# Context v of three heads by seven quarter products, and modulation sums by ScalarE and accumulating transfers

## The chip, the cores and the metric

The kernel runs on one core of a Trainium2 chip. The metric is device time in microseconds (us) of one execution. The engines of the core are named as the profile names them: PE (TensorE, the matmuls, with PEld for its weight loads), DVE (VectorE), ACT (ScalarE), POOL (GpSimd, which here only issues transfers) and SP (SyncE, which issues transfers too). Each engine takes its own instructions in order and waits for the others by semaphores.

## The reference, cut to what matters

Two layers over 512 latent tokens `x` and 256 context tokens `ctx`, of width 1024. Layer 0 is a bidirectional retention mixer with four heads, layer 1 a gated MLP in chunks. Each layer first normalizes its tokens and modulates them with a shift and a scale; a gate multiplies its output.

```python
shift_x, scale_x, gate_x = jnp.split(silu_c @ ada_w[i] + ada_b[i], 3, axis=-1)
hx = rmsnorm(x, norm_g[i]) * (1 + scale_x[:, None]) + shift_x[:, None]
hc = rmsnorm(ctx, norm_g[i]) * (1 + scale_c) + shift_c

def retention_project(h, w_in):
    q = to_heads(h @ w_in[:, :a], RET_HEADS)
    k = to_heads(h @ w_in[:, a:bq], RET_HEADS) * (RET_QK_DIM ** -0.5)
    v = to_heads(h @ w_in[:, bq:cq], RET_HEADS)
    z = h @ w_in[:, cq:]
```

Per head, q and k have 256 columns, v and z 512. For the latent tokens all four are computed, for the context tokens only k and v (the context's own output is needed by no later layer). The output is the latent stream after a final RMSNorm.

## The kernel before

**Precision.** A float32 matrix is held as a pair of fp32r tiles, high and low part: ACT casts the high part, DVE subtracts it from the source for the low part (`split`). One product of two such pairs is three matmuls (`mm3`: low x high, high x low, high x high).

**Quads and seven products.** The retention projections are done in quads: a matrix of weights cut into 2 x 2 quarters, against the tokens' matrix `A` cut the same way (512 tokens by 1024 features). A quad is computed by the Strassen-Winograd form: seven products of quarters in place of eight, with sums of weight quarters (built by DVE, in `Stream.sum`) and sums of token quarters (`S1` to `S4`, built once). The order in a quad is `SINGLE` = B11, T1, T2, B21, T3, B22, T4. `Product.run` runs one of them; the results are put together by ACT copies (`snap`) and DVE additions (`plus`), and `done` gets each finished quarter of the result. A latent product is 24 matmuls of 128x128 weights with 256 moving columns.

Twelve quads stand in `QUADS`. `("kq", h)` is k and q of a head; there the weights' tiles are what PE loads and the tokens move (`features`). `("vz", h, f)` is half f of the columns of v beside half f of z; there the tokens are loaded and the weights move (`tokens`). The first three quads (head 0) are done ahead; the loop at the end of the projection, `for n, q in enumerate(QUADS[3:])`, runs the other nine, n = 0 to 8: vz 1 (two), kq 1, vz 2 (two), kq 2, vz 3 (one), kq 3, vz 3 (one).

**The context.** `Product.beside` multiplies all 256 context tokens (`hc`) by the two raw quarters B11 and B21 of a quad: the left column of quarters, which is k in a kq quad and v in a vz quad. That is a plain product, 24 more matmuls behind each of B11 and B21.

**Weights.** `Stream` loads raw quarters (two transfers of 256 KB each, issued by SP) into seven slots, `w0` to `w6`, and makes the pairs two products ahead (`Q.get`) in four `hl` tiles.

**Order.** PE keeps the order of the text (`pe.kept`). In the projection loop ACT, DVE, SP and POOL have no written order; each queue's order is settled when the program is built. Work called by `aside` is pinned behind the instruction that stands before it in the text on ACT and DVE.

**The modulation of later stages** is computed in the background (`background`, one `step` per call): four pieces, i = 0 to 3, each a row vector `silu(c) @ W` with `W` 1024 x 1024. `ada_piece` loads eight rows of 128x1024 (512 KB each) into two buffers in turn, and DVE multiplies each by its column of `cpad` and adds it into `ada_a`. Its steps are one per row (nine in all), then an empty one; in the next, `columns` has PE sum over partitions (`pst<-ada_a,ones`), and one more finishes the piece. The first three pieces are done in the projection loop; before, a step follows each product except those of i = 2 and 4, from n = 0 on. The fourth follows during attention.

**Other names.** `between_modes` is one small float32 matmul of ones, put between two kinds of quads. `later` holds the finishing of k and q (rotation by `rope`, then `spill`), popped one at a time after some products. `spill` is a transfer to DRAM issued by POOL. `t2` are eleven buffers of 128x512 for snapshots. `decay` builds a head's decay table with Exp on ACT; head 0's is made in the loop at n = 5.

Of the kernel before, what the change touches and what calls it, by code (L numbers as in the profile page):

```python
# [13 lines left out]
P = 128  # L14
# [53 lines left out]
def hybrid_kernel(ctx, tc, xT_d, cT_d, cv_d, sv_d, rows_d, ada0_d, adag_d, w_d, rope_d, dec_d, ws_d, id_d, out_d):  # L68
# [86 lines left out]
    class Stream:  # L155
# [40 lines left out]
        def upto(self, n, late=None):  # L196

            while self.done < min(n, self.limit or len(self.items)):
# [4 lines left out]
                hl = place() if place else hl_tile(q[0] in ("vz", "v1"))  # L203
# [60 lines left out]
    def parts_of(q, u):  # L264
# [5 lines left out]
        if kind == "vz":  # L270
            return wide_parts(16 * i + (8 if nh else 4), kh, q[2])
        if kind == "v1":
            return wide_parts(64 + 4 * i, kh, nh)
# [4 lines left out]
    QUADS = (("kq", 0), ("vz", 0, 0), ("vz", 0, 1), ("vz", 1, 0), ("vz", 1, 1), ("kq", 1), ("vz", 2, 0), ("vz", 2, 1),  # L278
             ("kq", 2), ("vz", 3, 0), ("kq", 3), ("vz", 3, 1))
# [11 lines left out]
    for q in QUADS[3:]:  # L291
        Q.quad(q, SINGLE)
        for u in RAWS:
            Q.load((q, u), W, 1, parts_of(q, u))
# [79 lines left out]
    class Product:  # L374
# [3 lines left out]
        def __init__(self, product, done, side=None, z="tm"):  # L378
            self.product, self.done, self.side, self.z_tag, self.s = product, done, side, z, {}

# [9 lines left out]
        def beside(self, name, w):  # L390
# [5 lines left out]
            else:  # L396
                self.product(self.c, self.side[:, :, 4:8, :], w, False)
                self.done("c", self.c)

        def run(self, name, w):  # L400
# [22 lines left out]
            if name in ("B11", "B21"):  # L423
                self.beside(name, w)

# [211 lines left out]

    def project(q):
        if q[0] == "kq":
            return Product(features, kq_done(q[1]), hc)  # L640
        return Product(tokens, vz_done(q[1], q[2]), hc)
# [197 lines left out]

    spot = [0]  # L840
# [41 lines left out]
    def background():  # L882
        for i in range(4):
            a = None
            for a in ada_piece(i, *(("g1", ("g2", "g3")) if i < 3 else ("oA22", ("w2", "w3")))):
# [78 lines left out]
    def load_qk(h):  # L964
        tags = ("s0", "s1", "s2", "s3", "w4") if h % 2 == 0 else ("rope", "w5", "w6", "g2", "g3")
# [15 lines left out]
    def load_wo(h):  # L981
        raws = []
        for c in range(4):
            for j in range(len(raws), min(c + 2, 4)):
                raws.append(st([P, 1024], ("w0", "w7")[j % 2], name="raw"))
# [44 lines left out]
    dec0 = decay(0, ("g0", "s3"))  # L1030
# [607 lines left out]
```

## Time and profile before

| | |
|---|---|
| median of three timed runs | 871.4 us (870.92 to 871.57) |
| span of the profiled execution, first to last instruction | 869.6 us |
| transfers' queue 1 (issued by SP), share of the 16 DMA engines | 43.7% |
| transfers' queue 0 (issued by POOL) | 8.2% |

The profile gives the span of one execution; it has no time of its own beyond that, and the 1.8 us between the span and the median lie ahead of the first and behind the last instruction, or are the difference between executions. In the views, a row of a timeline is start, duration, engine, line, operation, tiles (out<-in), shape and count, with the idle time before it in brackets; a row of a group is count, busy time, mean ns of one and idle time before; a row of windows is, for each engine, busy us and instructions, then PE's clock, the DMA engines' share and GB/s; a row of DMA issues ends with the median us from issue to landing. Nearly all instructions carry line 54, that of a helper, so groups are told apart by tiles. `hl` are the pairs of weights, `oA` and `oS` those of latent tokens and their sums, `hc` those of the context.

### The profile page before, as it was taken

Reading aid. Unit: us, or ns where it says so; the run is one execution under the profiler, and the core shown is the slowest. Engines: PE = TensorE matmul, PEld = TensorE weight load, DVE = VectorE, ACT = ScalarE, POOL = GpSimd, SP = SyncE. Lnnn points to the kernel's source line nnn. Section 1 sums busy time; section 2 is a strip of 40 time slices with the busy share of each in tenths; the row PEclk is TensorE's granted clock in tenths of the full one; section 3 lists DMA queues with packets and bytes.
Section 4 is the critical chain, followed back from the end, with each engine's and each line's share of the span. In section 5 each row is a group of like instructions: output and inputs, shape, how many; then the busy total and the mean of one; then the engine's idle time right before and its main releaser. Section 6 shows DMA issues by size and latency. Waiting matters only on the chain.

```text
span 869.6 us, 16989 instructions
## 1 busy us (share of the span) xinstructions
PE 860.9 (99%) x6898; PEld 824.1 (95%) x6898; DVE 715.0 (82%) x1004; ACT 458.5 (53%) x711; POOL 58.3 (7%) x96
## 2 busy tenths in 40 slices
PE   8999999999999999999999999999999999999997
PEld 7899999999999999999989899999999899899986
DVE  4799988699789777878676679999899488688995
ACT  5476644435544346627363549744666456255434
POOL 0001210101102011000000002011000000000110
PEclk9999999999999999999999999999999999999999
DMA  9943887557567467746164602635435035035522
GB/s 359 404 152 109 256 279 254 170 181 242 203 213 256 132 219 302 267 165 241 66 222 141 215 4 110 211 117 206 135 122 193 26 122 203 16 122 170 120 46 102
DMA packets 74238, 153.81 MB, mean 177 GB/s; under 512 B 7728, under 2 KB 32816, under 8 KB 74160
## 3 DMA queue, kind: packets, MB, share of 16 engines
q1 hardware_dynamic: 65856, 128.40, 43.7%
q0 software_dynamic: 7872, 24.12, 8.2%
q8 instruction: 54, 0.88, 0.4%
q14 instruction: 24, 0.20, 0.1%
q10 hardware_dynamic: 432, 0.20, 0.1%
HBM read 128.58 MB, written 24.12 MB: 176 GB/s over the span
## 4 chain that ended last, share of the span: by engine, by line
PE 95%; DMA 3%; DVE 1%; ACT 0%; issue 0%; SPq 0%; DVEq 0%; ACTq 0%
PE pst L54 95%; DMA ada_w<-in_ada_dram 2%; DMA xs<-in_xT_dram 1%; DVE o L54 0%; ACT junk L54 0%; SPq L54 0%; ACT fss L54 0%; ACT o L54 0%; DVE fss L54 0%; ACT oA L54 0%; DVE oA L54 0%; DVE xs L54 0%; DVEq L1634 0%; DVE gs L54 0%; DVE ada_s L54 0%
## 5 line engine op out<-in xcount | busy, mean ns | idle before, releaser
L54 DVE TENSOR_TENSOR hl<-raw,hl 128x1024 fp32r<-128x1024 f32 (+2 forms) x197 | 235.4, 1199 | 65.9 <-ACT hl L54 65.3
L54 ACT CAST hl<-raw 128x1024 fp32r<-128x1024 f32 (+2 forms) x197 | 203.0, 1034 | 137.9 <-DVE raw L54 55.8
L54 PE MATMUL pst<-hl,oS 128*128 128x256 f32 x1152 | 133.9, 277 | 0.0
L54 PEld LDWEIGHTS pst<-hl,oS 128*128 128x128 f32 x1152 | 132.4, 188 | 0.4 <-issue 0.4
L54 PE MATMUL pst<-oS,hl 128*128 128x256 f32 x1104 | 132.5, 277 | 0.0
L54 PEld LDWEIGHTS pst<-oS,hl 128*128 128x128 f32 x1104 | 128.1, 188 | 0.8 <-issue 0.8
L54 PE MATMUL pst<-oA,hl 128*128 128x256 f32 x936 | 116.5, 279 | 0.1
L54 PEld LDWEIGHTS pst<-oA,hl 128*128 128x128 f32 x936 | 110.6, 188 | 2.3 <-issue 0.8
L54 DVE TENSOR_TENSOR raw<-raw 128x1024 f32<-128x1024 f32 x92 | 111.8, 1219 | 0.8
L54 ACT COPY snap<-pst 128x512 f32<-128x512 f32 x92 | 53.7, 584 | 92.7 <-PE pst L54 92.4
L54 PE MATMUL pst<-hl,oA 128*128 128x256 f32 x768 | 92.4, 277 | 0.0
L54 PE MATMUL pst<-og,hl 128*128 128x256 f32 x768 | 91.1, 278 | 0.0
L54 PEld LDWEIGHTS pst<-og,hl 128*128 128x128 f32 x768 | 89.2, 188 | 0.3
L54 PEld LDWEIGHTS pst<-hl,oA 128*128 128x128 f32 x768 | 89.4, 188 | 0.0
L54 PE MATMUL pst<-v,ph 128*128 128x512 f32 x192 | 59.8, 393 | 0.0
L54 PE MATMUL pst<-hl,ya 128*128 128x512 f32 (+1 forms) x246 | 59.1, 386 | 0.0
L54 PEld LDWEIGHTS pst<-hl,ya 128*128 128x128 f32 x246 | 45.3, 188 | 9.5
L54 DVE TENSOR_TENSOR snap<-pst,snap 128x512 f32<-128x512 f32 x69 | 47.3, 685 | 5.3 <-PE pst L54 5.3
L54 PE MATMUL pst<-hl,hc 128*128 128x256 f32 x384 | 46.1, 276 | 0.0
L54 PEld LDWEIGHTS pst<-hl,hc 128*128 128x128 f32 x384 | 44.7, 188 | 0.0
L54 ACT CAST ph<-pf 128x512 fp32r<-128x512 f32 x24 | 14.8, 618 | 54.5 <-DVE pf L54 54.1
L54 PEld LDWEIGHTS pst<-v,ph 128*128 128x128 f32 x192 | 36.1, 188 | 7.1
(186 smaller groups left out, 1022.7 us busy)
## 6 DMA issues: line engine op xcount, KB each, us to landing
raw<-in_w_dram SPq DMA_DIRECT2D x224, 256.0 KB, 4.1
bg<-in_adag_dram SPq DMA_DIRECT2D x32, 512.0 KB, 3.9
ada_w<-in_ada_dram SPq DMA_DIRECT2D x16, 512.0 KB, 8.7
raw<-in_w_dram SPq DMA_DIRECT2D x16, 512.0 KB, 4.3
bg<-in_dec_dram SPq DMA_DIRECT2D x12, 512.0 KB, 4.8
v<-snap POOLq DMA_DIRECT2D x16, 256.0 KB, 5.5
z<-snap POOLq DMA_DIRECT2D x16, 256.0 KB, 4.7
v<-v SPq DMA_DIRECT2D x8, 512.0 KB, 3.4
```

The source lines that it names most:

```text
L54: made = op(*args, **kw)
```

## The change

- The quads of heads 1 to 3 are cut otherwise: `("v", h)` is all 512 columns of v and `("z", h)` all of z, in place of two quads with half of each. The number of quads stays. Their order in the loop is kq 1, v 1, z 1, kq 2, v 2, z 2, v 3, z 3, kq 3.
- For these heads the context's v is computed in the seven-product form as well (`along`): context quarters `CA` of 128 tokens by 512 features, with their sums from `ctx_sums` (in the first quad of the loop), 12 matmuls behind each of the seven latent products of a v quad. The context's k, and v of head 0, stay as they were.
- `ada_piece` no longer adds on DVE. The first row is loaded into `ada_a` itself; ACT scales each row in place by its column of `cpad`; from the second row on, a transfer issued by POOL adds the row into `ada_a` (`accum_op=ALU.add`).
- Steps of the background follow every product from n = 1 on. Slots, tags and the places of `between_modes`, `later` and head 0's loads are moved to match: the weight slots `w4` and `w5` give way to `s0` and `s2`.

```diff
-    QUADS = (("kq", 0), ("vz", 0, 0), ("vz", 0, 1), ("vz", 1, 0), ("vz", 1, 1), ("kq", 1), ("vz", 2, 0), ("vz", 2, 1),
-             ("kq", 2), ("vz", 3, 0), ("kq", 3), ("vz", 3, 1))
+    QUADS = (("kq", 0), ("vz", 0, 0), ("vz", 0, 1), ("kq", 1), ("v", 1), ("z", 1), ("kq", 2), ("v", 2), ("z", 2), ("v", 3),
+             ("z", 3), ("kq", 3))
+    W2 = [w for w in W if w not in ("w4", "w5")] + ["s0", "s2"]
...
+        def along(self, name, w):
+
+            at, out = self.ctx
+            if name == "B11":
+                self.c, self.c_lo = pt(), t2("ctx")
+            elif name == "T1":
+                self.cz, self.c_hi = pt((P, HS)), t2("ctx")
+            bank = self.cz if name in ("T1", "B22") else self.c[:, HS:] if name == "B21" else self.c[:, 0:HS]
+            a = at[WITH[name]]
+            for kt in range(4):
+                r = (w[:, 0, kt * HS:kt * HS + HS], w[:, 1, kt * HS:kt * HS + HS])
+                mm3(bank, (a[:, 0, kt, :], a[:, 1, kt, :]), r, name in ("B11", "T1") and kt == 0, kt == 3)
+            lo, hi = ((t[:, 0:HS], t[:, HS:]) for t in (self.c_lo, getattr(self, "c_hi", self.c_lo)))
+            if name == "B11":
+                act.copy(lo[0], bank)
+            elif name == "T1":
+                act.copy(hi[1], bank)
+            elif name == "T2":
+                act.copy(lo[1], bank)
+            elif name == "B21":
+                dve.tensor_tensor(lo[0], bank, lo[0], ALU.add)
+            elif name == "B22":
+                dve.tensor_tensor(lo[1], bank, lo[1], ALU.add)
+                spill(out[:, 0, :], self.c_lo)
+            elif name == "T3":
+                dve.tensor_tensor(hi[1], bank, hi[1], ALU.add)
+            else:
+                act.copy(hi[0], bank)
+                spill(out[:, 1, :], self.c_hi)
...
+    def ctx_sums():
+        (x0, x1), (y0, y1) = ((c[:, :, 0:P], c[:, :, P:]) for c in cq)
+        dve.tensor_tensor(y1, x1, y1, ALU.add)
+        dve.tensor_tensor(shc, sh0[:, 0:4, 1], sh0[:, 4:8, 1], ALU.add)
+        t = ctx_tile("S1", "s1")
+        for k in range(4):
+            shifted(y1[:, k, :], shc[:, k:k + 1], t[:, 0, k, :], t[:, 1, k, :])
+        yield
+        dve.tensor_tensor(y1, y1, x0, ALU.subtract)
+        t = ctx_tile("S2", "w4")
+        for k in range(4):
+            shifted(y1[:, k, :], sh0[:, 4 + k, 1:2], t[:, 0, k, :], t[:, 1, k, :])
+        yield
...
@@ ada_piece
             if k < KT:
-                rows.append(bg_raw(tags))
+                rows.append(a if k == 0 else bg_raw(tags))
                 load(rows[k], adag_d[8 * i + k])
-            if k == 0:
-                yield None
-                continue
-            r, c = rows[k - 1], cpad[:, k - 1, 0:1]
-            if k == 1:
-                dve.tensor_scalar(a, r, c, None, ALU.mult)
-            else:
-                dve.scalar_tensor_tensor(a, r, c, a, ALU.mult, ALU.add)
+            if k:
+                r = rows[k - 1]
+                act.activation(r, r, AF.Copy, scale=cpad[:, k - 1, 0:1])
+                if k > 1:
+                    nc.gpsimd.dma_start(a, r, accum_op=ALU.add)
             yield None
...
     for n, q in enumerate(QUADS[3:]):
         pr = project(q)
-        if n in (0, 3, 6, 8):
+        if n in (1, 4, 6):
             inside_t.append(between_modes)
-        if n == 5:
+        if n == 3:
             inside.append(between_modes)
         for i, name in enumerate(SINGLE):
             pr.run(name, Q.get())
-            if i in (1, 5) if n == 0 else i % 2:
+            if i in (1, 5) if n == 0 else i % 2 or (n, i) == (8, 6):
                 popped()
-            if 2 not in pieces and i not in (2, 4):
+            if n == 0 and i % 2 == 0:
+                next(ctx_sum)
+            if n and 2 not in pieces:
                 pieces.append(step())
             if n == 5 and i % 2 == 0:
                 aside(dec0)
-            if n == 8 or (n == 6 and i < 3):
+            if n == 8 or (n == 7 and i < 3):
                 aside(qk0)
```

The finishing of v and z quarters follows the new quads (`wide_done`): of a v quad only the last quarter is copied by ACT, of a z quad all four get their SiLU there, the last one into a buffer of `t2`.

More of the change, by code (lines that the diff above doesn't have):

```diff
@@ L202, in upto @@
                 self.sum(self.done)
-                hl = place() if place else hl_tile(q[0] in ("vz", "v1"))
+                hl = place() if place else hl_tile(q[0] in ("vz", "v", "z", "v1"))
                 split((hl[:, 0, :], hl[:, 1, :]), r, late)
@@ L293, in hybrid_kernel @@
         for u in RAWS:
-            Q.load((q, u), W, 1, parts_of(q, u))
+            Q.load((q, u), W2, 1, parts_of(q, u))
     PROJECTED = len(Q.items)
@@ L837, in sum_s3, with ctx_tile @@
         kept_in("S3", f11)
+    shc = st([P, 4], "shb", name="shc")
+    def ctx_tile(key, tag):
+        CA[key] = st([P, 2, 4, P], tag, F32R, name="cs")
+        return CA[key]
+    def ctx_sums():
[11 more added lines that the diff above has]
+        yield
+        dve.tensor_tensor(y0, y0, y1, ALU.subtract)
+        t = ctx_tile("S4", "w5")
+        split((t[:, 0], t[:, 1]), y0)
+        yield
+        dve.tensor_tensor(x0, x0, x1, ALU.subtract)
+        t = ctx_tile("S3", "g3")
+        split((t[:, 0], t[:, 1]), x0)
+        yield
     spot = [0]
@@ L1029, in hybrid_kernel @@
     Q.free.remove("g0")
-    dec0 = decay(0, ("g0", "s3"))
+    Q.free += ["s0", "s2"]
+    Q.pump()
+    dec0 = decay(0, ("g0", "w7"))
+    ctx_sum = ctx_sums()
     pieces = []
```

32 lines of the change are left out of this document (26 added, 6 removed).

## The prediction

> **What bounds the kernel now.** I read the page first, then the projection stage, where the whole change lies, in three views: the table of windows, the timeline of weight loads, and the groups of instructions.
>
> ```profile
> span 869.6 us, 16989 instructions
> PE 860.9 (99%) x6898; PEld 824.1 (95%) x6898; DVE 715.0 (82%) x1004; ACT 458.5 (53%) x711; POOL 58.3 (7%) x96
> ...
> 67.00:330.00 263.00, 263.00 (x2319) 261.38 (x2318) 226.51 (x274) 127.26 (x164) 36.95 (x58) 1.00 0.64 214
> ```
>
> TensorE is busy 99% of the span. The third row is the stretch from 67 to 330 us: 263.00 of 263.00 us on PE, clock 1.00, DVE 226.51, ACT 127.26. Nothing that DVE, ACT or a transfer does there is seen by PE. So the time can fall only by matmuls that go, and it rises by whatever makes PE wait, us for us.
>
> ```profile
> 107.49 2.79 PEld L54 LDWEIGHTS pst<-hl,hc 128*128 128x128 f32 x24
> 110.21 5.51 PEld L54 LDWEIGHTS pst<-hl,oS 128*128 128x128 f32 x48
> 115.65 2.79 PEld L54 LDWEIGHTS pst<-hl,oA 128*128 128x128 f32 x24
> ...
> 151.01 2.79 PEld L54 LDWEIGHTS pst<-hl,oA 128*128 128x128 f32 x24
> 153.73 2.89 PEld L54 LDWEIGHTS pst<-oA,hl 128*128 128x128 f32 x24
> 156.56 2.90 PEld L54 LDWEIGHTS pst<-hc,hl 128*128 128x128 f32 x24
> 159.59 0.16 PEld L54 LDWEIGHTS pst<-ada_a,ones 128*32 128x32 f32 x8
> ```
>
> One product of a quad is 24 matmuls and takes 2.72 us from start to start (107.49 to 110.21), so 113.3 ns each. The row at 159.59 is `columns` of the first modulation piece: PE reads `ada_a` there, in the order of the text, with no wait.
>
> **The change, part by part.**
>
> *Context products.* Before, each of the two v/z quads of a head multiplies all the context by two v quarters: 2 x 24 matmuls, so 96 a head. After, seven products of 12 matmuls make 84. Three heads: 36 fewer, 36 x 113.3 ns = **-4.1 us**. These lie on the path.
>
> *Two smaller PE terms.* The loop has four `between_modes` matmuls in place of five.
>
> ```profile
> 179.46 0.78 PEld L54 LDWEIGHTS pst<-hl,oA 128*128 128x128 f32 x6
> 180.16 0.31 PEld L54 LDWEIGHTS pst<-ones 128*128 128x128 f32 x2
> 180.39 2.13 PEld L54 LDWEIGHTS pst<-hl,oA 128*128 128x128 f32 x18
> ```
>
> One takes 0.23 us (180.16 to 180.39): -0.2. But the feature quad behind a token quad at 153.73, which got none, ran its first 24 in 2.83 us, 0.11 more. After the change the quads kq 1 and kq 3 get none, 216 matmuls each: between 0 and 2 x 9 x 0.11 = 2.0 us; I take +1.0, as the columns' matmuls may end the effect early. Matmuls in all: **-3.3 us**.
>
> *Evacuation and the context's sums.* A head's two 512-wide ACT copies of context v give way to four 256-wide ones and three 256-wide DVE additions; `ctx_sums` adds seven 512-wide operations and sixteen small ones, over both engines, in the first quad of the loop.
>
> ```profile
> L54 DVE SCALAR_TENSOR_TENSOR ada_a<-bg,cpad,ada_a 128x1024 f32<-128x1024 f32 x28 | 35.8, 1279 | 0.6 <-DMA bg<-in_adag_dram 0.6
> ...
> L54 DVE TENSOR_TENSOR xs<-xs 128x512 f32<-128x512 f32 x8 | 5.2, 686 | 0.0
> ...
> L54 DVE SCALAR_TENSOR_TENSOR oS<-xs,shb,oS 128x256 fp32r<-128x256 f32 x4 | 1.7, 484 | 0.6 <-ACT oS L54 0.6
> ```
>
> On DVE that is five at 0.69 and eight at 0.48 or less: at most 7.3 us, in a quad that no longer has its five modulation steps of 1.28 us. DVE's slack hides it; price on PE 0. If that cover went, PE would lose the excess, about 1 us. Later quads lose all modulation work on DVE, which buys nothing, since PE waits for DVE nowhere here.
>
> *The modulation sums.* This is the term that decides. Before, step k of a piece was one DVE operation of 1.28 us. After, it is a scaling on ACT (k from 1 to 8) and, from the second on, a transfer by POOL that adds the row into `ada_a`: seven a piece, each writing the tile that the one before it writes. The weight rows still have two buffers, and a buffer is free for the next load only when its adding transfer has landed. Nothing in the trace is a 512 KB adding transfer. The nearest rows are:
>
> ```profile
> o<-x POOLq DMA_DIRECT2D x8, 256.0 KB, 4.0
> ...
> bg<-in_adag_dram SPq DMA_DIRECT2D x32, 512.0 KB, 3.9
> ...
> v<-v SPq DMA_DIRECT2D x8, 512.0 KB, 3.4
> ...
> DMA to landing us min/median/max: 3.8/4.0/5.5
> ...
> q0 software_dynamic: 1152, 2.10, 25.4%
> ...
> L54 ACT CAST hl<-raw 128x1024 fp32r<-128x1024 f32 x191 | 200.3, 1051 | 137.9 <-DVE raw L54 55.8 <-PE pst L54 51.9 <-issue 15.2
> ...
> L54 ACT CAST qk<-qk 128x512 fp32r<-128x512 f32 x20 | 12.4, 618 | 0.0
> ...
> L54 ACT ACTIVATE bg<-bg,lg 128x512 f32<-128x512 f32 x24 | 15.7, 715 | 11.4 <-DMA bg<-in_dec_dram 11.3
> ```
>
> The adding transfers `o<-x` at the end of the kernel move 256 KB and land after 3.8 to 5.5 us, 4.0 in the median. The q0 row is the window 800 to 850 us: these eight (2.10 MB) held all 16 DMA engines for 25.4% of 50 us, 12.7 us, so 1.6 us each. Twice the bytes add 1.6 us: estimate **5.6 us** per transfer. Below, no 512 KB transfer's median is under the 3.4 us of `v<-v`; above, the largest `o<-x` plus 1.6 us is 7.1. I take 5.6, from the nearest row, the one other adding transfer. The scaling of 1024 elements is estimated at 1051 + (715 - 618), so 1.15 us.
>
> Seven in a row take 7 x (5.6 + 0.1) = 39.9 us. The buffers give nearly the same: a round of transfer 5.6, load 3.9, scaling 1.15 and some 0.2 for handing over is 10.85 us for two rows; three rounds and the last transfer are 38.2. I use **40 us** from the first adding transfer until the piece is whole.
>
> How long has it? A step follows each product from quad n = 1 on. The first adding transfer belongs to step 2 of a piece and PE's `columns` to step 10. With token products of v at 36 x 113.3 ns = 4.08 us and all others at 2.72:
> - piece 1: four products of v 1 and four of z 1: 16.3 + 10.9 = 27.2 us
> - piece 2: the rest of kq 2 (19.0), half a doubled product ahead of it (2.7), two of v 2 (8.2): 29.9 us
> - piece 3: two of v 2 (8.2; its scaling stands behind a cast, not an evacuation, so nearly a product earlier) and all of z 2 (19.0): 27.2 us
>
> The scaling itself and the issue take 1.4 us off each: 25.8, 28.5, 25.8. PE takes its instructions in the order of the text, so it waits at `columns` for 40 less that: 14.2 + 11.5 + 14.2 = **+39.9 us**. At 3.4 us a transfer (buffers: 3 x 8.65 + 3.4 = 29.4) the waits are 3.6 + 0.9 + 3.6 = 8.1; at 7.1 us (7 x 7.2 = 50.4) they are 24.6 + 21.9 + 24.6 = 71.1. The fourth piece has its steps spread over attention, three to six a head, and costs nothing.
>
> A rule bears on this. The Trainium skill ("DMA: Bandwidth & Descriptors", section "Anatomy of one DMA — SWDGE (gpsimd) path") fits such a transfer at 2.0 us plus bytes over 436 GB/s, which for 256 KB is an estimate of 2.6 us and for 512 KB of 3.2; the trace's 4.0 for 256 KB of adding speaks against it here. By that figure the sum would be about +2.
>
> What is queued behind these waits: POOL holds the spills of q, k, v and z behind each adding transfer, so each may start up to 5.6 us late, and its `t2` buffer is held as long; eleven such buffers, of which I count eight or nine in use in v 1, hide that. SP holds the weight loads behind each row load. That is covered:
>
> ```profile
> SPq L54 <- DVE ada_a L54: 84.7, 22, 13.2
> ...
> L54 ACT COPY snap<-pst 128x512 f32<-128x512 f32 x92 | 53.7, 584 | 92.7 <-PE pst L54 92.4
> ...
> L54 ACT ACTIVATE snap<-snap 128x512 f32<-128x512 f32 x16 | 10.1, 630 | 12.0 <-DVE snap L54 12.0
> ...
> L54 ACT ACT_TABLE_LOAD x16 | 20.5, 1283 | 1.9 <-PEq L1627 1.7
> ```
>
> SP, in the view of its own waits from 60 to 345 us, already stood up to 13.2 us at a time for `ada_a`, and PE lost nothing. ACT gets 24 x 1.15 = 28 us in the loop and has 136 us of slack in the window quoted above; its tight place is a rival below, worked out from the last three rows and those of the casts and exponentials above.
>
> **Sum.** -3.3 + 39.9 = +36.6 us: the profiled span goes from 869.6 to 906.2. The median of the three timed runs is 871.4, 1.8 us above the span, so the prediction is **908.0 us**.
>
> **Rivals.**
> - *As short as a plain transfer.* Adding costs nothing over moving, 3.4 us: +8.1 - 3.3 = +4.8, so 876.2. For it: the source lies in SBUF, not in HBM. Against it: 4.0 us for half the bytes. The figure of the Trainium skill's page named above belongs to this case and would make it about 874 (an estimate: 3 x 8.45 + 3.2 = 28.6 us a piece).
> - *ACT becomes the bound in z 2.* Quad z 2 has 19.0 us on PE. ACT has seven casts (7.4), three snaps (1.8), four SiLUs (2.5), five scalings (5.8), six exponentials of `decay` (4.3), and SiLU and Exp in turn need some four table loads at 1.28 (5.1): 26.9 us. The excess of 7.9, less a lead of one to two products (2.7 to 5.4), costs 2.5 to 5.2; with the chain of transfers barely late, about 880. For it: before, decay shared a quad with kq, with no SiLU inside. Against it: alone it is small, and a PE that waits for `ada_a` gives ACT the time anyway.
> - *The chain is hidden; faster.* If a piece is whole in 26 to 28 us, PE never waits and only the matmuls count: 871.4 - 3.3 = **868.1**. It decides at 7 x 3.7 = 25.9, so a transfer of 3.7 us, with loads near their fastest as well. Against it: no row of an adding transfer is below 3.8, at half the size.
> - *Much longer under load.* The DMA engines are 0.64 busy in the window quoted first; a row more costs some 3.2 us of them (twice 1.6), which may stretch loads and transfers to 7.1 us: +71.1 - 3.3, so 939.
>
> **How the numbers follow.** The waiting chain near 5.6 us: 0.52. Longer, up to 939 and a little beyond: 0.10. As short as a plain transfer: 0.12. ACT as the bound: 0.08. Hidden: 0.14 faster by over 0.2% (about 1.7 us, what a measurement here can tell from no change), and 0.04 within. So 0.14, 0.04 and 0.82. The range reaches from the hidden case, 867, to 7.1 us a transfer, 940: it leaves out some 0.1.
>
> **What would show it.** In the timeline of PE's weight loads: three waits of 11 to 14 us ahead of `pst<-ada_a` and none elsewhere in the loop; adding transfers `ada_a<-bg` at 5 to 6 us to landing, with POOL waiting between them; SP waiting for those transfers; 36 fewer context matmuls at 113 ns. If the adding transfers land in under 3.8 us, or POOL sends them without waiting for each other and the row loads are ahead, the chain falls, and so does the forecast. If PE waits for `hl` instead, ACT's order is the cause.

## The result, and the profile after

The changed kernel takes 969.9 us (median of four runs, 964.74 to 970.34) where the kernel before takes 871.2 (870.92 to 871.57): a ratio of 1.1117, interval 1.1091 to 1.1143. The forecast was 908.0 us, range 867 to 940. The direction was right, the size was not.

The head of the page after, then the same stretch of 263 us as before in the table of windows:

```profile
span 968.6 us, 17017 instructions
PE 877.4 (91%) x6860; PEld 836.3 (86%) x6860; DVE 689.7 (71%) x996; ACT 499.2 (52%) x760; POOL 82.5 (9%) x124
```

```profile
67.00:330.00 263.00, 197.10 (x1634) 193.90 (x1632) 160.57 (x210) 123.68 (x157) 45.59 (x64) 0.87 0.71 201
```

PE, full before, is busy for 197.10 of 263.00 us and its clock falls to 0.87 there. DVE and ACT are less busy than before too (160.57 for 226.51; 123.68 for 127.26). So no engine became the bound; the engines wait for something that is none of them. PE's waits say for what (us in total, times, longest):

```profile
PE pst L54 <- DMA ada_a<-bg: 61.7, 3, 28.7
PE pst L54 <- ACT snap L54: 6.9, 2, 5.0
PE pst L54 <- DVE pl L54: 6.1, 2, 5.1
PE pst L54 <- DVE snap L54: 4.0, 2, 2.9
```

Three waits, 61.7 us together, are at `columns`. Here is each of the first three pieces of the modulation: POOL's row of its first adding transfer, then PE's row of its `columns` (start, duration; the bracket is the idle time before):

```profile
147.16 0.88 POOL L939 DMA_DIRECT2D ada_a<-bg  x1
...
213.79 0.92 POOL L939 DMA_DIRECT2D ada_a<-bg  x1 [3.41 <-ACT bg L54]
...
276.99 0.91 POOL L939 DMA_DIRECT2D ada_a<-bg  x1 [1.73 <-ACT bg L54]
```

```profile
196.88 1.08 PE L54 MATMUL pst<-ada_a,ones 128*32 128x256 f32 x8 [18.12 <-DMA ada_a<-bg]
...
262.78 1.08 PE L54 MATMUL pst<-ada_a,ones 128*32 128x256 f32 x8 [14.85 <-DMA ada_a<-bg]
...
337.00 1.08 PE L54 MATMUL pst<-ada_a,ones 128*32 128x256 f32 x8 [28.70 <-DMA ada_a<-bg]
```

From the first of seven adding transfers to `columns` it took 49.7, 49.0 and 60.0 us: 7.1, 7.0 and 8.6 us for each row. The time to landing of all 28, in the view of line 939:

```profile
DMA to landing us min/median/max: 4.5/6.7/11.4
```

**Where the 99.0 us of the span went** (968.6 less 869.6). PE's idle time over the whole span rose by 99.0 - 16.5 = 82.5 us, since its busy time rose by 16.5 (877.4 less 860.9). Of this, 61.7 is at `columns` and 20.8 is elsewhere. PE's timeline has most of the second part: 9.8 us in the loop behind ACT's late rows (waits of 5.00 and 1.93 for ACT, and 2.85 for a DVE that had itself waited for ACT), 6.1 for `pl` in attention, 2.3 for `acc`, and 1.2 for DVE at the start of the loop. The largest of those in the loop:

```profile
171.45 4.59 PE L54 MATMUL pst<-hl,oS 128*128 128x256 f32 x24 [5.00 <-ACT snap L54]
```

The busy time rose although 38 matmuls are gone (6898 less 6860; 4.3 us at 113.3 ns), so the others took 16.5 + 4.3 = 20.8 us longer; that this is 20.8 once more is chance. Most of it is the clock: PE's busy time in windows of 1 us, each times what the granted clock lacks to 1.00 there, adds up to 16.0 us (0.0 before). The rest, 4.8, we read as the pace shown under the first experiment. The windows around the first wait, and PE's timeline behind it:

```profile
180.00:197.00 17.00, 0.12 (x4) 0.15 (x8) 8.33 (x10) 3.85 (x5) 3.55 (x5) 0.55 0.92 255
197.00:207.00 10.00, 10.00 (x69) 9.19 (x69) 3.83 (x6) 2.30 (x4) 0.69 (x1) 0.74 0.42 139
```

```profile
197.90 5.00 PE L54 MATMUL pst<-hl,oS 128*128 128x256 f32 x24
202.74 0.38 PE L54 MATMUL pst<-ident,cole 128*128 128x128 f32 x2
```

The clock fell to half while PE stood, and stayed there when work came back: the first 24 matmuls took 4.84 us from start to start (197.90 to 202.74) in place of 2.72, and the ten microseconds behind the wait ran at 0.74. This wait cost its length and then some 2.6 us more (10 x 0.26). The Trainium skill ("TensorE: Matmul & The Clock Gate", section "Part 1: The HAM clock gate (the "warmup" mystery)") has the clock go to half after an idle window of about 3.4 us and back after a busy one of that length; the trace agrees with it in kind, but doesn't show the figure itself: in windows of 0.5 us the clock is at half from 181.6 to 202.2 us, so it fell some 2.9 us after PE's last matmul (178.8) and came back some 5.3 us after PE went on (196.9).

### The profile page after: what moved, and what is told of

The parts are those of the page before. It is cut to its first block, busy times and chain, and to the rows that moved or that the text cites. A ratio compares the mean times of both kernels' runs of the same rounds, so it can differ in the third digit from the quotient of the medians.

```text
span 968.6 us, 17017 instructions
## 1 busy us (share of the span) xinstructions
PE 877.4 (91%) x6860; PEld 836.3 (86%) x6860; DVE 689.7 (71%) x996; ACT 499.2 (52%) x760; POOL 82.5 (9%) x124
## 5 line engine op out<-in xcount | busy, mean ns | idle before, releaser
L54 PE MATMUL pst<-hl,oS 128*128 128x256 f32 x1152 | 141.3, 284 | 6.9 <-ACT snap L54 6.9
L54 PEld LDWEIGHTS pst<-hl,oS 128*128 128x128 f32 x1152 | 138.7, 194 | 8.9 <-ACT snap L54 7.3
L54 PE MATMUL pst<-oA,hl 128*128 128x256 f32 x936 | 119.3, 283 | 2.9 <-DVE snap L54 2.9
L54 PEld LDWEIGHTS pst<-oA,hl 128*128 128x128 f32 x936 | 113.4, 192 | 4.8 <-DVE snap L54 3.0
L54 PE MATMUL pst<-hl,oA 128*128 128x256 f32 x768 | 96.0, 282 | 1.4 <-DVE snap L54 1.2
L54 PEld LDWEIGHTS pst<-hl,oA 128*128 128x128 f32 x768 | 92.6, 192 | 2.7 <-ACT hl L54 1.3
L54 ACT COPY snap<-pst 128x512 f32<-128x512 f32 x80 | 46.5, 583 | 60.4 <-PE pst L54 60.3
L54 ACT ACTIVATE bg<-bg,cpad 128x1024 f32<-128x1024 f32 x28 | 32.2, 1152 | 65.5 <-DMA bg<-in_adag_dram 65.3
L54 PE MATMUL pst<-ada_a,ones 128*32 128x256 f32 x24 | 3.2, 631 | 61.7 <-DMA ada_a<-bg 61.7
L54 PE MATMUL pst<-v,pl 128*128 128x512 f32 x96 | 39.2, 408 | 6.1 <-DVE pl L54 6.1
```

Source lines behind the costliest of these rows:

```text
L54: made = op(*args, **kw)
```

## The experiments

Two theories stood at the start. *Theory 1*, the prediction's: the time lies in the chain of adding transfers that PE waits for, and the context products are a small gain. *Theory 2*: ACT now scales the rows in its own order, so late rows hold up the casts and evacuations that stand behind them; the transfers are one way to make rows late. All kernels below are the changed kernel with the edit that is shown, unless another base is named; `...` in an edit stands for lines left out. Times from single runs are given without an interval; the kernel before took 871.3 to 871.9 us in the median beside each.

### The two halves of the change alone

`ctx_only` keeps the context products and puts the sums back on DVE, with their rows:

```diff
-                rows.append(a if k == 0 else bg_raw(tags))
+                rows.append(bg_raw(tags))
...
-                act.activation(r, r, AF.Copy, scale=cpad[:, k - 1, 0:1])
-                if k > 1:
-                    nc.gpsimd.dma_start(a, r, accum_op=ALU.add)
+                dve.scalar_tensor_tensor(a, r, c, a, ALU.mult, ALU.add)
```

> The modulation sums go back to DVE operations (a multiply and seven multiply-adds a piece, rows in two buffers); everything else is as after the change. Theory 1 (the chain of adding transfers makes PE wait at columns, and nothing else of the change costs): the three waits ahead of pst<-ada_a of 18.1, 14.9 and 28.7 us go, with the clock loss behind them, and the time is that of before less the matmul terms, 866 to 869 us, ratio 0.994 to 0.998. Theory 2 (the new context products or their evacuation make PE wait too): 875 us or more, with waits ahead of hl,cs or hl,hc.

884.06 us (882.62 to 885.23), ratio 1.0146 [1.0132, 1.016]. The half that was to gain 3.3 us costs 12.5. It isn't the context products alone, though. The change puts a step of the modulation behind every product, and here each step that has a row is a DVE operation of 1.28 us: up to seven a quad, where before had up to five and the changed kernel has none on DVE. PE's and DVE's timelines where the first loss lies:

```profile
176.07 1.08 PE L54 MATMUL pst<-ada_a,ones 128*32 128x256 f32 x8 [4.17 <-DVE snap L54]
```

```profile
173.00 0.68 DVE L54 TENSOR_TENSOR rope_a<-pst,rope 128x512 f32<-128x512 f32 x1
...
174.20 1.22 DVE L54 TENSOR_TENSOR hl<-raw,hl 128x1024 fp32r<-128x1024 f32 x1
175.34 0.68 DVE L54 TENSOR_TENSOR snap<-pst,snap 128x512 f32<-128x512 f32 x1
```

`columns` waits 4.17 us, and `ada_a` isn't what it waits for: the releaser is a `snap` addition that empties a PSUM bank (where matmuls leave their results), and it stands on DVE behind rotations and a `hl`. (`columns` takes a bank of the tag that quads use; that this bank is the one that `snap` left is read from the code.) It lies in z 1, where a product lasts 2.7 us and no context matmul follows, so DVE has less time to catch up than in v 1; DVE works there without a pause from 162.8 us on, and two of the modulation's multiply-adds are in that stretch. The second part of the loss is the pace. In the timeline of weight loads, 24 matmuls in this kernel and in `ctx_modes`, an experiment further down:

```profile
230.84 2.90 PEld L54 LDWEIGHTS pst<-hl,oS 128*128 128x128 f32 x24
233.67 1.49 PEld L54 LDWEIGHTS pst<-hl,cs 128*128 128x128 f32 x12
```

```profile
230.25 2.79 PEld L54 LDWEIGHTS pst<-hl,oS 128*128 128x128 f32 x24
232.97 1.44 PEld L54 LDWEIGHTS pst<-hl,cs 128*128 128x128 f32 x12
```

The first pair is of `ctx_only`, the second of `ctx_modes`: 2.83 us against 2.72, so 118 ns a matmul against 113. This is a token quad, and the transposes of piece 2's `columns` lie just ahead of it (225.87 us): without a `between_modes` behind them the slow pace holds for quads on end, here over some 140 us of the loop, which makes some 5 us (0.11 in each 2.83). With the waits (4.17, and 1.15 and 1.39 in two other places), 2.9 us of lower clock (counted as above) and 4.3 us of matmuls saved, that is some 10.7; the loop ended 11.0 us later than before (first `pst<-qk` at 340.92 for 329.90).

`sums_only` is the other half: the kernel before with the new modulation sums, rows and all.

```diff
-                rows.append(bg_raw(tags))
+                rows.append(a if k == 0 else bg_raw(tags))
...
-                dve.scalar_tensor_tensor(a, r, c, a, ALU.mult, ALU.add)
+                act.activation(r, r, AF.Copy, scale=cpad[:, k - 1, 0:1])
+                if k > 1:
+                    nc.gpsimd.dma_start(a, r, accum_op=ALU.add)
```

> The kernel before with the modulation sums alone by ScalarE and adding transfers; its steps stay at five of seven products, from n = 0 on. Between step 2 and step 10 PE then has about 11 products of 3.5 us, 39 us, in place of 26 to 28. Theory 1 (a chain of 49 us a piece against PE's time between those steps): three waits of about 10 us ahead of pst<-ada_a, some 10 us more of clock and of the fourth piece, 905 to 920 us. Theory 2 (ACT's load, table loads included, is the cause, not the chain): the SiLU and Exp no longer meet in one quad, so little is lost, 875 us or less.

931.92 us, above what either theory expected, and PE's waits show why theory 1 isn't all:

```profile
PE pst L54 <- ACT snap L54: 17.6, 4, 6.5
PE pst L54 <- DMA ada_a<-bg: 12.4, 3, 6.0
```

With the steps spread as before the change, PE waits for `ada_a` only 12.4 us in three places, and yet the kernel loses 60. It waits longer for ACT, 17.6 us.

### Theory 2: ACT behind late rows

`late_columns` gives each of the first three pieces six more steps before PE reads it:

```diff
             yield
+            for _ in range(6 if i < 3 else 0):
+                yield
             if i == 0:
```

> After the change, with six empty steps put ahead of columns in each of the first three pieces, so that PE reads ada_a six products later; the transfers are the same. Theory 1: six products are 19 us or so, and the chain needs 22 more than it has: the waits ahead of pst<-ada_a fall from 18.1, 14.9 and 28.7 us to under 10 in all, and 875 to 890 us remain, of which 8 us are attention's waits on the fourth piece. Theory 2 (ACT stands behind late rows and keeps back the casts that PE needs): PE waits for hl or snap in the loop instead, and the time stays above 930 us.

924.42 us, between the two theories. No wait at `ada_a` is left, and the time is still 53 us above that of before. ACT's timeline, then PE's, then ACT's waits:

```profile
167.25 1.05 ACT L54 CAST hl<-raw 128x1024 fp32r<-128x1024 f32 x1
170.86 1.15 ACT L54 ACTIVATE bg<-bg,cpad 128x1024 f32<-128x1024 f32 x1 [2.55 <-DMA bg<-in_adag_dram]
171.91 0.57 ACT L54 COPY snap<-pst 128x512 f32<-128x512 f32 x1
```

```profile
172.53 4.38 PE L54 MATMUL pst<-hl,oS 128*128 128x256 f32 x24 [5.83 <-ACT snap L54]
```

```profile
ACT bg L54 <- DMA bg<-in_adag_dram: 73.3, 15, 8.5
```

ACT stands 2.55 us for a row of weights; the copy that empties a PSUM bank stands behind the scaling; PE waits 5.83 us for that copy. The row was late since its buffer was still being read by an adding transfer: that one was issued at 161.23 us and landed 5.7 us later, the row's load was issued at 167.0 and landed 3.8 us later. The changed kernel has the same sequence at its wait of 5.00 us. So the chain of transfers reaches PE by two ways, and taking away one leaves the other.

### What of it is adding, what is moving, what is ACT

`add_on_dve` keeps ACT's scaling and adds on DVE; no adding transfer is left. `plain_copy` keeps the transfers and lets them overwrite (the additions are left out).

```diff
-                    nc.gpsimd.dma_start(a, r, accum_op=ALU.add)
+                    dve.tensor_tensor(a, a, r, ALU.add)
```

> After the change, with each transfer ada_a<-bg replaced by a DVE addition of the scaled row into ada_a; ACT still scales. Theory 1 (the transfers' chain is what costs; ACT's scaling as such does not): as the context change alone, 882 to 890 us. Theory 2 (ACT's extra 28 us of scaling, with the table loads in z 2, holds back PE's casts even when the rows come in time): 900 us or more, with PE waiting for hl or ACT snap.

```diff
-                    nc.gpsimd.dma_start(a, r, accum_op=ALU.add)
+                    nc.gpsimd.dma_start(a, r)
```

> After the change, with the transfers ada_a<-bg as plain copies; the additions of the modulation sums are left out (only the last row stays). Theory A (adding is what makes these transfers long, by the engine time that the o<-x rows show): they land in 3.5 to 4.5 us in the median in place of 6.7, the chain shrinks to about 33 us, and the waits at columns fall to some 5, 3 and 12 us, 895 to 905 us. Theory B (traffic beside them and the hand-over on POOL's queue): they still land in 5.5 us or more, and the time stays above 935 us.

`add_on_dve` takes 892.91 us, just above theory 1's range, and `plain_copy` 936.21, theory B's time with a landing between the two theories. The copies land after:

```profile
DMA to landing us min/median/max: 2.9/5.2/7.7
```

That is a ladder: 871.6 before; 884.1 in `ctx_only` (+12.5); 892.9 with ACT's scaling (+8.8); 936.2 with transfers that only move (+43.3); 969.9 with transfers that add (+33.7). Its steps are not separate costs that would add up in another order: `ctx_only` and `add_on_dve` have modulation work on DVE, the last two kernels have none. Adding makes a transfer 1.5 us longer (6.7 for 5.2; over the 21 of the first three pieces alone 6.7 for 4.9), which over 21 is 31.5 to 38 us, about the last step of the ladder: each of them is in a chain that PE waits for. Moving alone costs more than that.

`two_sums_three_buffers` cuts the chain in the first two pieces: two accumulators by turns, three row buffers, one DVE addition at the end.

```diff
+        b = st([P, D], "g0", name="ada_b") if i < 2 else None
...
-                    nc.gpsimd.dma_start(a, r, accum_op=ALU.add)
+                    nc.gpsimd.dma_start(a if b is None or k % 2 else b, r, accum_op=ALU.add)
...
+        if b is not None:
+            dve.tensor_tensor(a, a, b, ALU.add)
```

> After the change, in the first two pieces: odd rows added into ada_a, even rows into a second tile, joined by one DVE addition, and three row buffers in place of two, so that two adding transfers can be under way and a row can load meanwhile. The third piece is unchanged. Theory 1 (one adding transfer waits for the landing of the one before, 7.1 us a row): the chain of a piece falls from 49 us to about 30, the waits at columns from 18.1 and 14.9 us to under 5 each, the third stays near 28; 930 to 945 us. Theory 2 (the DMA engines are full, so that two transfers at once take twice as long each): landings near 12 us, the waits stay above 12 us, over 955 us.

942.73 us, inside the range of its theory 1, but not as that had it. The waits at `columns` of the first two pieces fell from 18.12 and 14.85 to 9.27 and 11.47, not under 5; the third, which has one accumulator, still waits 27.2:

```profile
PE pst L54 <- DMA ada_a<-bg: 27.2, 1, 27.2
PE pst L54 <- DVE ada_a L54: 11.5, 1, 11.5
PE pst L54 <- DVE snap L54: 10.4, 2, 9.3
```

The 9.27 us, too, are a wait for the chain: the addition that joins the two sums stood 6.10 us on DVE for the last transfer, and the `snap` addition that `columns` needs stood behind it. The chain of the first piece took 33.5 us, from 145.95 to that addition at 179.44, in place of 49.7. Two transfers at once did not take twice as long: 7.1 us to landing in the median, so theory 2 falls.

`late_four` puts four row buffers into the first two pieces of `late_columns`, to give ACT its rows in time:

```diff
-            for a in ada_piece(i, *(("g1", ("g2", "s3")) if i < 3 else ("oA22", ("w2", "w3")))):
+            for a in ada_piece(i, *(("g1", ("g2", "s3", "g0", "w7") if i < 2 else ("g2", "s3")) if i < 3 else ("oA22", ("w2", "w3")))):
```

> As late_columns, with four row buffers in place of two in the first two pieces; the adding transfers still wait for one another. Theory (late_columns still lost 21 us between 130 and 290 us because ACT, in order, stood before scalings whose rows could not load until an adding transfer had landed): rows come in time, PE's waits for ACT snap and hl there fall under 8 us, and the time is some 12 to 20 us below late_columns, 904 to 912 us. Rival (the serial adding transfers themselves, or POOL's late spills, hold PE back): the waits there stay near 20 us and the time at 920 us or more.

925.40 us against 924.42: a miss in time, and a confounded one. ACT's waits from 130 to 290 us:

```profile
ACT bg L54 <- DMA bg<-in_dec_dram: 15.7, 1, 15.7
ACT bg L54 <- DMA bg<-in_adag_dram: 12.9, 3, 5.3
```

ACT's waits for modulation rows fell to 12.9 us there (40.0 in `late_columns`), and PE's waits for ACT's `snap` from 11.3 to 1.0, as theory 2 has it. But the two new buffers are those of `decay`'s rows, which then came late: ACT stood 15.7 us for one, and PE 15.7 us behind it. The gain was given back; for the waits this bears theory 2 out, for the time nothing follows.

### Why a transfer took 6.7 us

The forecast had 5.6. `rows_once` leaves out five of the eight row loads of each of the first three pieces (the two buffers are scaled and added again), so that no row loads beside the last transfers of a piece. `half_rows` makes of each adding transfer two of 256 KB, each with its own half of `ada_a`.

```diff
-                rows.append(a if k == 0 else bg_raw(tags))
-                load(rows[k], adag_d[8 * i + k])
+                rows.append(a if k == 0 else rows[k - 2] if k > 2 and i < 3 else bg_raw(tags))
+                if k < 3 or i == 3:
+                    load(rows[k], adag_d[8 * i + k])
```

> As after, but in the first three pieces only the first three of eight rows are loaded; the two buffers are scaled and added again and again (five row loads a piece are left out, and the values with them). Theory that the row loads running beside the adding transfers stretch them: landing falls from 6.7 to 5.5 us or less in the median, a row of the chain costs 6 us or less, waits at columns fall to 6 to 12 us each, 925 to 945 us. Rival, that the length is the adding transfer's own (read, read, add, write) or comes from the weight loads: landing 6.3 to 6.9 us, time 960 to 970.

```diff
-                    nc.gpsimd.dma_start(a, r, accum_op=ALU.add)
+                    for s in (slice(0, HS * 2), slice(HS * 2, D)):
+                        nc.gpsimd.dma_start(a[:, s], r[:, s], accum_op=ALU.add)
```

> As after, but each adding transfer of 512 KB is two of 256 KB, one for each half of the accumulator, issued one behind the other. Theory that most of the 6.7 us is fixed (issue, latency, completion): each half lands after 4.5 to 5.5 us, the two overlap, a row of the chain costs 5.5 to 6.3 us, 935 to 955 us. Rival, that it is a price per byte or that the halves follow each other on one queue: the second half lands 6.5 us or later after the first was issued, a row costs 7 us or more, 965 to 985 us.

`rows_once`, 941.20 us, inside its theory's range, with waits at `columns` of 16.66, 4.01 and 9.80 us where 6 to 12 each were expected: the view of the transfers' line, POOL's timeline and PE's.

```profile
DMA to landing us min/median/max: 4.5/5.3/11.4
```

```profile
147.58 0.89 POOL L940 DMA_DIRECT2D ada_a<-bg  x1
...
205.67 0.93 POOL L940 DMA_DIRECT2D ada_a<-bg  x1 [3.42 <-ACT bg L54]
```

```profile
188.97 1.08 PE L54 MATMUL pst<-ada_a,ones 128*32 128x256 f32 x8 [16.66 <-DMA ada_a<-bg]
...
247.40 0.64 PE L54 MATMUL pst<-ada_a,ones 128*32 128x256 f32 x8 [4.01 <-DMA ada_a<-bg]
```

Without the row loads beside them the transfers land after 5.3 us (4.9 over the 21 of the first three pieces), and the first two chains take 41.4 and 41.7 us in place of 49.7 and 49.0: close to the forecast's 40. So about 1.1 us of a row's 7.1 goes when the row loads go. And the kernel still takes 941 us, 33 over the forecast: the excess lies not in the transfer alone.

`half_rows`, 968.62 us: the rival held. Were most of a transfer's time fixed, the halves would have overlapped and a row would have become shorter; it did not. The halves land after

```profile
DMA to landing us min/median/max: 3.2/5.7/10.1
```

and the first chain ends as before, from its first issue at 146.88 to the second half of `columns` at 196.16:

```profile
146.88 1.76 POOL L940 DMA_DIRECT2D ada_a<-bg  x2
```

```profile
196.16 1.07 PE L54 MATMUL pst<-ada_a,ones 128*32 128x256 f32 x4 [2.79 <-DMA ada_a<-bg]
```

A row costs 7.0 us whole or halved. Whether it is the bytes or the one queue that sets it, the two runs can't tell.

### The context part, mended

From here on the base is `ctx_only`: DVE adds the rows. `ctx_modes` also puts `between_modes` into kq 1 and kq 3 and behind the transposes of `columns` of pieces 2 and 3.

```diff
                 yield from columns(a, sh1)
+                inside_t.append(between_modes)
...
                 yield from columns(a, gs1)
+                inside_t.append(between_modes)
...
-        if n == 3:
+        if n in (0, 3, 8):
             inside.append(between_modes)
```

> The context change alone (ctx_only), with between_modes matmuls added: one in the first product of kq 1 and of kq 3, and one in the first token product behind the transposes of the second and the third piece. Theory (token and feature products run at 2.83 us in place of 2.72 from such a point until the next small float32 matmul, which cost ctx_only 5.3 us over 100 to 132, 226 to 265 and 270 to 341 us): 4 to 5 us less than ctx_only, 879 to 880 us. Rival (the 2.83 is a mark of those quads and no matmul ends it): the time of ctx_only plus 0.9 us for four more matmuls, 885 us.

883.32 us (882.43 to 884.88), ratio 1.0134 [1.0119, 1.015]: no difference from `ctx_only` that the intervals show, and not the 4 to 5 us that were expected, though the pace went from 118 to 113 ns (the rows above). PE came to the third `columns` sooner and waited there longer, 3.54 us in place of 1.39:

```profile
265.33 0.64 PE L54 MATMUL pst<-ada_a,ones 128*32 128x256 f32 x8 [3.54 <-DVE ada_a L54]
```

```profile
265.01 0.64 PE L54 MATMUL pst<-ada_a,ones 128*32 128x256 f32 x8 [1.39 <-DVE ada_a L54]
```

The first row is of `ctx_modes`, the second of `ctx_only`: PE starts at nearly the same time, and what the faster matmuls had gained turned into waiting. What they gained behind it went to the clock, since the longer wait was followed by matmuls at half clock, 18 in 3.45 us (267.03 to 270.48):

```profile
267.03 3.53 PEld L54 LDWEIGHTS pst<-hl,oA 128*128 128x128 f32 x18
```

So the slow pace is no cost of its own here: with DVE behind, ending it gained nothing that can be told from noise.

`ctx_steps` therefore also moves the steps, so that `columns` falls elsewhere, pins `ctx_sums`, and has its `between_modes` at fixed quads, not behind the transposes (the edit is against `ctx_only`):

```diff
-        if n in (1, 4, 6):
+        if n in (1, 4, 5, 7):
             inside_t.append(between_modes)
-        if n == 3:
+        if n in (0, 3, 8):
             inside.append(between_modes)
...
-                next(ctx_sum)
-            if n and 2 not in pieces:
+                aside(ctx_sum)
+            if n and 2 not in pieces and not (n in (1, 2, 5) and i in (2, 4)):
```

> The context change alone, with between_modes in kq 1, kq 3, v 1, z 2, kq 2, v 2's successor and z 3, the context's sums pinned behind the text on ACT and DVE, and four steps left out (i = 2 and 4 of n = 1, 2 and 5) so that columns stands at n = 3 i = 0, n = 4 i = 5 and n = 6 i = 5, where no two other products hold the tm banks. Theory (ctx_only loses 8 us in waits at columns with their clock, most of it for a tm bank that DVE has yet to empty, 5.3 us in slow products and 1.2 us at the start of the loop): 866 to 869 us, less than before the change. Rival (DVE is the bound of z quads): waits for hl or snap in z 1 and z 2 remain, 873 us or more.

872.74 us (872.21 to 874.61), ratio 1.0016 [1.0007, 1.0025]: 11.3 us of the 12.5 come back, by several edits at once, but the 866 to 869 us that were expected are not reached. What is left stands in PE's waits:

```profile
PE pst L54 <- DVE ctx L54: 2.2, 1, 2.2
PE pst L54 <- ACT hl L54: 1.2, 1, 1.2
```

The second lies at 257 us, where ACT had waited 3.44 us for `decay`'s rows and then changed its table for the exponentials and back for SiLU, two loads of 1.28 us: the prediction's rival of ACT in z 2, at a small size. `ctx_dec` is `ctx_steps` with `decay` made two quads earlier, and `ctx_dec_pop` is `ctx_dec` with `later` emptied ahead of attention, not in it:

```diff
-            if n == 5 and i % 2 == 0:
+            if n == 3 and i % 2 == 0:
                 aside(dec0)
```

> As ctx_steps, with head 0's decay table made beside kq 2 (n = 3) in place of z 2 (n = 5), so that Exp and SiLU are not asked of ACT in turn. Theory (the 4.3 us of PE waits that ctx_steps has left, at 256 to 276 us, come from ACT's table loads and its wait for decay's rows in z 2): they go, and the time is 867 to 869.5 us, less than before the change. Rival (z 2 and v 3 are short of DVE, whatever stands beside them): waits of 3 us or more remain there, 872 us or more.

```diff
+    while later:
+        popped()
     drained(dec0)
...
-            while later:
-                popped()
```

> As ctx_dec, with the finishing of the last k and q quarters ahead of attention again, as before the change, in place of behind its first scores. Theory (attention lost 1.1 us in ctx_steps, by DVE's queue at its first scores: from pst<-qk to pst<-hl_e 199.8 us against 198.7 before): 1 us less than ctx_dec. Rival (the last quad is kq 3 now, and its finishing stands in the way wherever it is put): the same time as ctx_dec or more.

`ctx_dec` takes 871.27 us (868.55 to 873.14), ratio 0.9995 [0.9987, 1.0004], no difference and not the gain that was expected, with a scatter of 4.6 us where before has 1.2. `ctx_dec_pop` takes 873.15 (871.80 to 876.84), ratio 1.002 [1.001, 1.0031]; its rival held. PE waits at attention's first products, in a profile of its longest execution:

```profile
333.70 2.50 PE L54 MATMUL pst<-qk 128*128 128x256 f32 x10 [2.77 <-DVE pf L54]
```

`ctx_paced` is `ctx_dec` with a step behind five of the seven products of a quad, as before the change, with the `between_modes` of the changed kernel's token quads again, and with the loading of head 0's k and q four products later:

```diff
-        if n in (1, 4, 5, 7):
+        if n in (1, 4, 6):
             inside_t.append(between_modes)
...
-            if n and 2 not in pieces and not (n in (1, 2, 5) and i in (2, 4)):
+            if n and 2 not in pieces and i not in (2, 4) and (n, i) != (5, 0):
...
-            if n == 8 or (n == 7 and i < 3):
+            if n == 8 or (n == 7 and i > 3):
```

> As ctx_dec (the context products alone, modulation sums on VectorE), but feature and modulation work goes into five of the seven products' steps of a piece instead of all, so that the rows of ada_w have more time to come in. Theory: ctx_dec's scatter (868.6 to 873.1 us) comes from rows that are wanted every product and come late for VectorE in some executions; with fewer wants they are in time: 867.5 to 869.5 us, scatter of at most 2 us, faster than before (871.5). Rival: the scatter comes from VectorE's own load in the loop, or from work that now stands closer to the attention's start: 870 to 873 us, no different from before or slower.

868.86 us (867.93 to 870.14), ratio 0.997 [0.9958, 0.9982]: 0.3% faster than before, the only version here that is, with a scatter of 2.2 us.

```profile
PE 856.6 (99%) x6864; PEld 819.3 (95%) x6864; DVE 723.4 (83%) x1028; ACT 461.4 (53%) x724; POOL 57.9 (7%) x96
```

```profile
67.00:330.00 263.00, 263.00 (x2316) 261.38 (x2315) 235.16 (x293) 132.13 (x180) 36.15 (x57) 1.00 0.70 224
```

PE is full again in the whole stretch, and its busy time is 4.3 us under before's 860.9. That late rows made `ctx_dec`'s scatter fits this result, but its slower executions weren't profiled and three things were edited, so it isn't shown.

## Why the prediction was right in kind and wrong in size

The sum gave the span +36.6 us, and it rose by 99.0. Of the 62.4 us between them, 21.8 lie in the term at `columns` (61.7 for 39.9), 20.8 in waits elsewhere that the sum put at nothing, and 19.8 in matmuls that ran slower (20.8 us for the +1.0 of the pace).

- **The chain of adding transfers at `columns`, +39.9 us:** the mechanism was right and is the largest term, 61.7 us. The first step that failed is its size. A row was put at 5.7 us and took 7.0 to 7.1 in the first two pieces: the 5.6 was about right without row loads beside it (41.4 and 41.7 us a chain), and the row loads add 1.1. The third piece took 60.0 us, since in two places the next transfer wasn't ready when the one before had landed: 6.9 us from 281.6, where the scaling stood on ACT behind casts and copies that waited for PE, and 6.6 from 325.7, where its row was still loading. The three chains took 158.7 us in place of 120, but PE, held up on the way, also came to `columns` later: it had 97.0 us on the way in place of 80.1.
- **PE saturated, waits cost one for one:** right, with a part missing. Each longer wait also costs what PE then loses at half clock, some 2.6 us behind the first and 16.0 us in all. The sum had no such term.
- **Context products, -4.1 us:** right as a price of work; `ctx_paced`, with no waits in the loop, is 4.3 us shorter in PE's busy time and 3.0 in its median. **"Evacuation and the context's sums ... price on PE 0", about 1 us if the cover went:** the cover went, and PE waited 1.2 us for DVE at the start of the loop, also in the changed kernel; `ctx_sums` has six wide operations on DVE, not five. The 12.5 us of `ctx_only` are no measure of this term, since DVE there has the modulation work that the change takes from it. They show what a slack that is a mean over 263 us hides: `columns` sits in z 1, where DVE is behind (4.17 us). **The slow pace, +1.0,** was counted for kq 1 and kq 3 alone, with the columns' matmuls as what might end it; behind the transposes of pieces 2 and 3 it began instead. We read 4.8 us of the changed kernel's slower matmuls as this pace.
- **ACT has slack; waits for rows are covered:** the second step that failed, and one that the length of a transfer alone does not explain (9.8 us of PE's waits in the loop). ACT's 136 us of slack in the window says nothing of its order: a scaling whose row is late holds the casts and copies behind it. `late_columns` has no wait for `ada_a` and still loses 53 us. `add_on_dve`, with the same scalings on ACT and no transfers, loses only 8.8 over `ctx_only`, and ACT waits 24.1 us for modulation rows in it (73.3 in `late_columns`).
- **"The fourth piece ... costs nothing":** wrong. ACT's timeline in attention, then SP's waits from 440 to 500 us:

```profile
486.54 1.04 ACT L54 CAST hl<-raw 128x1024 fp32r<-128x1024 f32 x1 [9.17 <-DMA raw<-in_w_dram]
```

```profile
SPq L54 <- DMA ada_a<-bg: 31.3, 5, 10.2
```

  SP stands for a buffer that an adding transfer still reads, the weights behind it on SP come late, ACT waits 9.17 us for them, and PE waits for `pl` (6.1 us in the rows on the result). `add_on_dve` has no such wait, `plain_copy` has one of 5.0: it comes from the transfers, adding or not. The prediction had SP's stand-still as covered, since before it was up to 13.2 us at a time in the loop and PE lost nothing.
- **Rivals.** The plain-transfer case fell: copies alone land after 5.2 us, not 3.4. (The 3.4 was not the lowest median of a 512 KB transfer, either: the view of transfers before has one `wsT<-in_ws_dram` at 3.1.) "Much longer under load" was the right case for the length of a row (7.1 us was its figure), and still gave 939: it put more at `columns` than was lost there (71.1 for 61.7) and nothing on waits elsewhere and on the clock.

## What to carry to other kernels

A sum moved from an engine into a chain of transfers must be priced by what it holds: its row buffer, the next load of that buffer, the queue that issues this load, and the engine that waits in order for the row. Slack read as a mean over a stage hides no instruction with a place in the order; look at the busy time of the other engines in the few products around the instruction that PE will wait for. And where PE is full, an edit that saves matmuls is worth its price only once the work that other engines do per product has been spread to suit: here the same 36 matmuls gave +12.5 us or -3.0, by where the steps, `between_modes`, `ctx_sums` and `decay` stood.

## What the runs showed that was not expected

- Adding 512 KB from one buffer to another took at least 4.5 us, 5.3 in the median with most row loads left out and 6.7 with them; a plain copy beside the same row loads took 5.2. Two halves of 256 KB, issued together, took as long as the whole (7.0 us a row).
- Matmuls of 113 ns ran at 118 for quads on end, behind two of three transposes of `columns` in `ctx_only` and behind a change of the kind of quad, and at 113 again where `between_modes`, a small float32 matmul, was put there. Why is not shown.
